# Starting the input projection with two of five token tiles, in a two-layer diffusion step on one core

## The chip, the cores and the metric

The kernel runs on one core of a Trainium2 chip. The metric is the device time of one execution in microseconds (us). The core has five engines that run their own instruction queues in order: TensorE (PE in the rows; PEld is its weight load), VectorE (DVE), ScalarE (ACT), GpSimd (POOL) and SyncE (SP), which issues most of the loads.

## The reference

Two layers work on 128 context tokens and 512 latent tokens of 1024 features. Layer 0 is latent attention, layer 1 a gated MLP. The part that the change touches is the head of layer 0:

```python
def modulation(cond, w_mod, b_mod):
    m = (jax.nn.silu(cond) @ w_mod + b_mod).reshape(-1, 1, 3 * D_MODEL)
    return m[..., :D_MODEL], m[..., D_MODEL:2 * D_MODEL], m[..., 2 * D_MODEL:]
...
        sh_l, sc_l, g_l = modulation(c, w_mod[layer], b_mod[layer])
        hl = rmsnorm(xl, norm_g[layer]) * (1.0 + sc_l) + sh_l
...
def mla_project(h, w_in, q_norm_g, kv_norm_g, w_uq):
    proj = h @ w_in
    c_q = proj[..., :Q_RANK]
    c_kv = proj[..., Q_RANK:Q_RANK + KV_RANK]
```

The input x is normalised per token, scaled and shifted per feature with values that come from the conditioning vector (one set for context, one for latent tokens), and multiplied with w_in. Behind it follow attention, the MLP layer, and a last norm.

## The kernel before

The 640 tokens are five token tiles of 128 (tile 0 is the context), the 1024 features are eight feature tiles. Every matrix product of the projection is made of three float32r products: a matrix is split into a high half (cast on ScalarE) and a low half (the rest, on VectorE) by `split` (L143), and `mm3` (L148) adds high by high, high by low and low by high.

The head works in four kinds of steps.

- The norm of a token tile: squares with their sum on ScalarE (L303), two small steps for the reciprocal root on VectorE and GpSimd (`rstd`, L154), scaling on VectorE (L306).
- Turning: TensorE turns the normalised tile, eight 128x128 blocks per token tile (L316), into `xnT`, where features lie on partitions; ScalarE and VectorE copy it out of PSUM.
- Modulation: the scale and shift of the feature tiles come in six pieces (`PIECES`, L202: four of one feature tile, two of two). `mod_piece` (L213) loads w_mod, 1 MB for one feature tile, and multiplies it with silu(c) (L225); `mod_cols` (L234) copies the resulting rows out of PSUM (L238), turns them with TensorE (L240), reduces them to columns and adds bias and gain (L245, L254, L261). `conditions` (L284) makes silu(c) from rows of all small vectors, which TensorE turns first (L286).
- The projection: `h_piece` (L331) applies scale and shift to the feature tiles of a piece (L337) and splits the result into halves; `load_tok` (L275) loads and splits 832 columns of w_in for one feature tile; `tok_mm` (L353) multiplies one token tile with it, 512 columns (q), and 320 more (kv) for tokens 0 and 1. Five token tiles times eight feature tiles add up in PSUM.

Before the change, the order in the code is: all five x loads among the small rows; the five norms; piece 0 of the modulation and token weights 0; the turning of all five tiles; then for each piece in turn the modulation and h of the *next* piece, ahead of the products of this one:

```python
for q, (k0, nk) in enumerate(PIECES):
    ks = range(k0, k0 + nk)
    if q + 1 < len(PIECES):
        mod_piece(*PIECES[q + 1], True)
        mod_cols(*PIECES[q + 1])
        h_piece(*PIECES[q + 1])
        ...
        for t in range(NT):
            tok_mm(t, ks, 0)
```

The instructions of an engine stand in the order that a scheduling layer makes from this program; each engine works them off in order, waiting where its operands are not there. Loads issued by SP go through eight semaphores in turn: a load waits on SP until the one eight loads earlier has landed, and until the place that it overwrites is free. `raw` and `raw2` are rings of places for loaded weights; `raw2` lies on the places of the x tiles.

Of the kernel before, what the change touches and what calls it, by code (L numbers as in the profile page):

```python
# [9 lines left out]
AF = mybir.ActivationFunctionType  # L10
# [84 lines left out]
def _program(tc, nc, i, o, sb, ps, dr):  # L95
# [22 lines left out]
    def R(a, n):  # L118
        return arR[:, a : a + n]

    def F(a, n):
        return arF[:, a : a + n]
# [11 lines left out]
    def dtile(name):  # L134
        while turn[0] % 4 in held:
            turn[0] += 1
        a = turn[0] % 4 * 1024
        turn[0] += 1
        return arP[:, a : a + 1024]
# [34 lines left out]
    def load_x(t):  # L174
        nc.sync.dma_start(F(F_X + t * D, D), x_src[t])

    def load_rows(name, at, n):
        src = i[name]
        src = (
            src.rearrange("(k p) -> k p", p=P)  # L180
            if len(src.shape) == 1
            else src.rearrange("a (k p) -> (a k) p", p=P)
        )
        nc.sync.dma_start(arF[at : at + n, F_MOD : F_MOD + P], src)

    load_x(0)
    load_rows("c", C_C, 8)
# [1 line left out]
    load_x(1)  # L189
    load_rows("b_mod", C_BMOD, 48)  # L190
    load_rows("norm_g", C_NG, 16)
    load_x(2)
    load_rows("mlp_v_norm_g", C_VG, 16)
    load_rows("mlp_v_norm_b", C_VB, 16)
    load_rows("attn_q_norm_g", C_QG, 4)
    load_x(3)
    load_x(4)
    make_identity(nc, ident)
    V.memset(nhalf, -0.5)

# [12 lines left out]
    def mod_piece(k0, nk, second):  # L213


        n = 2 * nk * P
        for kk in range(2):
            a = (raw2 if second and kk else raw).take(4 * n)
            for part in range(2):
                nc.sync.dma_start(  # L220
                    F3(a, 4 * n, a=4)[:, :, part * nk * P : (part + 1) * nk * P],
                    wmod(0, part * D + k0 * P, nk * P, 4 * kk, 4),
                )
            for j in range(4):
                T.matmul(  # L225
                    arP[32 * j : 32 * j + 32, 3584 : 3584 + n],
                    s32[:, 4 * kk + j, :],
                    F(a + j * n, n),
                    start=kk == 0,
                    stop=kk == 1,  # L230
                    tile_position=(0, 32 * j),
                )
# [40 lines left out]
    wtok = []  # L273

    def load_tok(k):  # L275
        a = (raw2 if k else raw).take(TCOLS)
        nc.sync.dma_start(F(a, TCOLS), i["attn_w_in"][0, k * P : (k + 1) * P, :TCOLS])
        w = ring.take(2 * TCOLS)
        wtok.append((R(w, TCOLS), R(w + TCOLS, TCOLS)))
        if k:  # L280
            split(*wtok[k], F(a, TCOLS))
        return F(a, TCOLS)

    def conditions():  # L284
        pc = dtile("pc")
        T.transpose(pc[:, :C_N], cr[:C_N], ident[:C_N, :C_N])  # L286
        V.tensor_copy(cst, pc[:, :C_N])

        cc = cst[:, C_C : C_C + 16]
        th = col(16)  # L290
        S.activation(th, cc, AF.Tanh, scale=0.5)
        V.scalar_tensor_tensor(silc, th, 1.0, cc, ALU.add, ALU.mult)
        V.tensor_scalar(silc, silc, 0.5, None, ALU.mult)

        V.memset(s32, 0.0)
        V.tensor_copy(s32[:, :, 0:2], silc.rearrange("p (c k) -> p k c", c=2))


    xnT = F3(F_Y, 5120, a=KD)
    for t in range(NT):  # L300
        x = F(F_X + t * D, D)
        ss = col()
        mark = S.activation(F(F_Y + t * D, D), x, AF.Square, accum_out=ss)  # L303
        r = col()
        rstd(r, ss, D)
        V.tensor_scalar(x, x, r, None, ALU.mult)  # L306
        if t == 3:
            with tc.issue_after(mark.ins):
                conditions()
    mod_piece(*PIECES[0], False)  # L310
    first = load_tok(0)
    for t in range(NT):
        x = F(F_X + t * D, D)
        pt = arP[:, t % 3 * 1024 : t % 3 * 1024 + 1024]
        for k in range(KD):
            T.transpose(pt[:, k * P : (k + 1) * P], x[:, k * P : (k + 1) * P], ident)  # L316
        dst = xnT[:, :, t * P : (t + 1) * P]
        pt = pt.rearrange("p (k n) -> p k n", n=P)
        if t == 1:
            V.tensor_copy(dst, pt)  # L320
        elif t > 2:
            S.copy(dst[:, :4], pt[:, :4])
            V.tensor_copy(dst[:, 4:], pt[:, 4:])
        else:
            S.copy(dst, pt)

    def hT(k):
        a = R_HT + k * 1280
# [211 lines left out]
        nc.sync.dma_start(d_gate[layer].rearrange("c k p -> (c k) p"), gro)  # L540


    mod_cols(*PIECES[0])
    h_piece(0, 1, 0, 2)
    split(*wtok[0], first)
    h_piece(0, 1, 2, NT)
    for q, (k0, nk) in enumerate(PIECES):
        ks = range(k0, k0 + nk)
        if q + 1 < len(PIECES):
            mod_piece(*PIECES[q + 1], True)  # L550
            mod_cols(*PIECES[q + 1])
            h_piece(*PIECES[q + 1])
            for k in range(PIECES[q + 1][0], sum(PIECES[q + 1])):
                load_tok(k)
            for t in range(NT):
                tok_mm(t, ks, 0)
                if t < 2:
                    tok_mm(t, ks, 1)
    nc.sync.dma_start(kvg, i["attn_kv_norm_g"].partition_broadcast(P)[:, 0, :])
    for t in range(NT):  # L560
        tok_mm(t, ks, 0)
# [947 lines left out]
```

## Time and profile before

| | |
|---|---|
| runs | 825.76, 826.68, 829.06 us; median 826.68 |
| the profiled execution | 829.0 us; its span from first to last instruction 827.2 us |
| TensorE busy over the span | 801.7 us (97%) |
| VectorE, ScalarE, GpSimd busy | 650.9, 405.5, 44.2 us |
| TensorE's granted clock, mean | 0.995 of full speed |
| loads and stores | 131.13 MB |

The profile is that of one execution. A start in its rows is counted from the start of the span, and a row of a timeline names engine, line, operation and what ended the idle time ahead of it. Pipelined matmuls overlap, so their durations add up to more than the time from one start to the next.

### The profile page before, as it was taken

The numbers are of one execution on the slowest core, as the hardware profiler recorded it, in microseconds if no ns is written. First come the engines' busy times: TensorE is split into PE (matmuls) and PEld (weight loads), VectorE is DVE, ScalarE is ACT, GpSimd is POOL, SyncE is SP. The second block draws the span as 40 slices with busy tenths as digits, with TensorE's granted clock in tenths as the row PEclk, the third lists the DMA queues.
The fourth block names the chain that finished last, engine by engine and source line by source line (L and its number), as shares of the span: only waits on it lengthen the run. The fifth ranks groups of instructions, "written<-read, shape, count | busy, mean of one in ns | idle before, by whom it ended". The sixth has DMA issues, their size and how long they took to land.

```text
span 827.2 us, 12759 instructions
## 1 busy us (share of the span) xinstructions
PE 801.7 (97%) x4874; PEld 732.2 (89%) x4874; DVE 650.9 (79%) x1145; ACT 405.5 (49%) x718; POOL 44.2 (5%) x68
## 2 busy tenths in 40 slices
PE   4999999999999999999999999999999999999996
PEld 3679999999999998887888889899999999888886
DVE  4664998899999798468978759899999997885332
ACT  5334334677666685245322358346564546533111
POOL 1001000000000000001000011100001011200010
PEclk9999999999999999999999999999999999999998
DMA  9981557022115046538869646643444657754111
GB/s 275 333 264 32 179 140 229 2 74 88 57 52 153 3 137 201 193 104 280 257 188 272 192 166 217 199 148 112 128 150 116 188 177 246 251 191 140 64 70 70
DMA packets 105301, 131.13 MB, mean 159 GB/s; under 512 B 5564, under 2 KB 69592, under 8 KB 104984
## 3 DMA queue, kind: packets, MB, share of 16 engines
q1 hardware_dynamic: 102152, 119.77, 46.3%
q0 software_dynamic: 3088, 10.55, 4.0%
q8 instruction: 38, 0.62, 0.3%
q14 instruction: 23, 0.19, 0.1%
HBM read 106.78 MB, written 23.52 MB: 158 GB/s over the span
## 4 chain that ended last, share of the span: by engine, by line
PE 67%; DVE 16%; DMA 9%; issue 5%; ACT 2%; POOL 1%; SPq 0%; POOLq 0%; DVEq 0%; ACTq 0%
PE arP L1218 20%; PE arP L150 13%; PE arP L152 12%; PE arP L151 12%; DVE arR L146 4%; PE arP L756 4%; DVE arF L492 3%; DMA arF<-in_w_mod 3%; DMA arF<-d_h 3%; PE arP L784 1%; PE arP L1275 1%; PE arP L1276 1%; DMA arR<-d_vh 1%; DVE st L768 1%; PE arP L225 1%
## 5 line engine op out<-in xcount | busy, mean ns | idle before, releaser
L150 PE MATMUL arP<-arR 128*128 128x512 f32 (+3 forms) x840 | 298.1, 356 | 1.7 <-DVE arR L146 1.4
L152 PE MATMUL arP<-arR 128*128 128x512 f32 (+3 forms) x840 | 295.8, 353 | 0.0
L151 PE MATMUL arP<-arR 128*128 128x512 f32 (+3 forms) x840 | 295.8, 352 | 0.0
L145 ACT CAST arR<-arF 128x1024 fp32r<-128x1024 f32 (+4 forms) x199 | 164.3, 854 | 160.8 <-PE arP L1218 25.9
L146 DVE TENSOR_TENSOR arR<-arF,arR 128x1024 fp32r<-128x1024 f32 (+4 forms) x199 | 190.4, 974 | 38.0 <-ACT arR L145 33.9
L1218 PE MATMUL arP<-arR 128*128 128x320 f32 x1344 | 202.5, 311 | 0.9 <-DVE arF L1306 0.9
L1218 PEld LDWEIGHTS arP<-arR 128*128 128x128 f32 x1344 | 199.1, 189 | 1.2 <-DVE arF L1306 1.1
L150 PEld LDWEIGHTS arP<-arR 128*128 128x128 f32 x840 | 158.0, 188 | 23.5 <-DVE arR L146 2.6
L152 PEld LDWEIGHTS arP<-arR 128*128 128x128 f32 x840 | 157.9, 188 | 18.4
L151 PEld LDWEIGHTS arP<-arR 128*128 128x128 f32 x840 | 158.0, 188 | 18.1 <-issue 0.8
L492 DVE SCALAR_TENSOR_TENSOR arF<-arF,silc 128x512 f32<-128x512 f32 x112 | 78.4, 743 | 0.8 <-DMA arF<-in_w_mod 0.6
L146 DVE TENSOR_TENSOR arR<-arP,arR 128x512 fp32r<-128x512 f32 (+4 forms) x86 | 54.9, 684 | 9.1 <-ACT arR L145 8.8
L756 PE MATMUL arP<-arR 128*128 128x320 f32 (+1 forms) x360 | 54.9, 309 | 0.2 <-DVE arR L719 0.2
L145 ACT CAST arR<-arP 128x512 fp32r<-128x512 f32 (+4 forms) x86 | 46.0, 605 | 17.4 <-PE arP L152 13.4
L756 PEld LDWEIGHTS arP<-arR 128*128 128x128 f32 x360 | 51.9, 188 | 0.8 <-DVE arR L719 0.4
L772 ACT ACTIVATE arF<-arP,st 128x640 f32<-128x640 f32 (+1 forms) x40 | 28.0, 702 | 14.3 <-DVE st L771 13.9
L1420 DVE TENSOR_TENSOR arF<-arP,arF 128x512 f32<-128x512 f32 (+1 forms) x11 | 6.8, 637 | 33.2 <-PE arP L152 33.2
L157 POOL TENSOR_TENSOR st<-st,nhalf 128x1 f32<-128x1 f32 x15 | 11.0, 734 | 407.6 <-DVE st L156 333.6
L776 ACT ACTIVATE arF<-arF,st 128x640 f32<-128x640 f32 (+1 forms) x40 | 28.9, 742 | 5.2 <-DVE st L775 4.1
L768 DVE TENSOR_REDUCE st<-arP 128x1 f32<-128x640 f32 (+1 forms) x40 | 28.0, 709 | 2.5 <-PE arP L756 2.3
L1422 ACT ACTIVATE arF<-arF 128x512 f32<-128x512 f32 (+1 forms) x11 | 6.5, 589 | 45.4 <-DVE arF L1421 45.4
L1047 ACT ACTIVATE arF<-arP 128x512 f32<-128x512 f32 x20 | 11.7, 592 | 26.4 <-PE arP L152 22.4
(160 smaller groups left out, 698.1 us busy)
## 6 DMA issues: line engine op xcount, KB each, us to landing
arF<-in_mlp_w_in SPq DMA_DIRECT2D x48, 512.0 KB, 4.5
arF<-in_w_mod SPq DMA_DIRECT2D x40, 512.0 KB, 4.8
arF<-in_mlp_w_o SPq DMA_DIRECT2D x32, 256.0 KB, 4.4
d_t<-arF SPq DMA_DIRECT2D x16, 320.0 KB, 3.4
arR<-d_vh POOLq DMA_DIRECT2D x8, 640.0 KB, 6.4
arF<-in_x_sample SPq DMA_DIRECT2D x8, 512.0 KB, 5.2
arF<-in_w_mod SPq DMA_DIRECT2D x16, 256.0 KB, 6.1
arF<-in_attn_w_in SPq DMA_DIRECT2D x8, 512.0 KB, 4.3
```

The costliest lines, as they stand in the source:

```text
L145: S.copy(h, x)
L146: V.tensor_tensor(l, x, h.bitcast(F32), ALU.subtract)
L150: T.matmul(out, a[0], b[0], start=start, stop=False)
L151: T.matmul(out, a[0], b[1], start=False, stop=False)
L152: T.matmul(out, a[1], b[0], start=False, stop=stop)
L492: V.scalar_tensor_tensor(acc[:, c, :], w, sc, acc[:, c, :], ALU.mult, ALU.add)
L756: T.matmul(p[:, n0 : n0 + n], a[:, qs], b[:, c0 : c0 + n], start=s0, stop=s1)
L768: V.tensor_reduce(c[:, 0:1], sc, AX.X if q == 0 else AX.XY, ALU.max)
L772: S.activation(pv, sc, AF.Exp, bias=c[:, 0:1], scale=SCALE, accum_out=c[:, 1:2])
L776: S.activation(pr, pr, AF.Identity, scale=c[:, 2:3])
L1047: S.activation(vt, p, AF.Gelu_apprx_tanh)
L1218: T.matmul(out, x, y, start=first and k + j == 0, stop=k == 3 and j == 2, skip_group_check=True,)
```

## The change

The head is written out in another order, with loads, norms and turning of x spread over it:

- x tiles 2, 3 and 4 are loaded behind w_mod and w_in for feature tile 0 (tile 2) and 1 (tiles 3 and 4).
- Three small row loads go from SP's queue to GpSimd's.
- `mod_piece` becomes a load (`mod_load`) and products (`mod_mm`), so that pieces 1 and 2 can be loaded ahead.
- `x_tile` holds norm and turning of one token tile. Its squares go to a scratch place of `arR`. Every tile is copied out of PSUM in halves by both engines.
- Token tiles 0 and 1 are turned first; feature tile 0 is then multiplied with token tiles 0 to 2, feature tile 1 with token tiles 0 to 2, and both with tiles 3 and 4 at the end. From piece 2 on the loop is the old one.

```diff
     load_rows("b_mod", C_BMOD, 48)
     load_rows("norm_g", C_NG, 16)
-    load_x(2)
-    load_rows("mlp_v_norm_g", C_VG, 16)
-    load_rows("mlp_v_norm_b", C_VB, 16)
-    load_rows("attn_q_norm_g", C_QG, 4)
-    load_x(3)
-    load_x(4)
+    load_rows("mlp_v_norm_g", C_VG, 16, nc.gpsimd)
+    load_rows("mlp_v_norm_b", C_VB, 16, nc.gpsimd)
+    load_rows("attn_q_norm_g", C_QG, 4, nc.gpsimd)
...
     def load_tok(k):
-        a = (raw2 if k else raw).take(TCOLS)
+        a = (raw if k in (0, 2) else raw2).take(TCOLS)
...
-        if k:
+        if k > 2:
             split(*wtok[k], F(a, TCOLS))
...
-    for t in range(NT):
+    scaled = []
+
+    def x_tile(t):
+
         x = F(F_X + t * D, D)
         ss = col()
-        mark = S.activation(F(F_Y + t * D, D), x, AF.Square, accum_out=ss)
+        S.activation(R(R_G + t % 2 * D, D), x, AF.Square, accum_out=ss)
         r = col()
-        rstd(r, ss, D)
-        V.tensor_scalar(x, x, r, None, ALU.mult)
...
+        if t:
+            with tc.issue_after(scaled[-1].ins):
+                rstd(r, ss, D)
+        else:
+            rstd(r, ss, D)
+        scaled.append(V.tensor_scalar(x, x, r, None, ALU.mult))
...
+    at = [mod_load(*PIECES[0], False)]
+    wf = [load_tok(0)]
+    load_x(2)
+    x_tile(0)
+    conditions()
+    x_tile(1)
+    at.append(mod_load(*PIECES[1], True))
+    wf.append(load_tok(1))
+    load_x(3)
+    load_x(4)
+    mod_mm(1, at[0])
     mod_cols(*PIECES[0])
     h_piece(0, 1, 0, 2)
-    split(*wtok[0], first)
-    h_piece(0, 1, 2, NT)
+    split(*wtok[0], wf[0])
+    for t in range(2):
+        tok_mm(t, [0], 0)
+        tok_mm(t, [0], 1)
+    x_tile(2)
+    h_piece(0, 1, 2, 3)
+    tok_mm(2, [0], 0)
+    at.append(mod_load(*PIECES[2], True))
+    wf.append(load_tok(2))
+    mod_mm(1, at[1])
+    mod_cols(*PIECES[1])
+    h_piece(1, 1, 0, 3)
+    split(*wtok[1], wf[1])
+    for t in range(3):
+        tok_mm(t, [1], 0)
+        if t < 2:
+            tok_mm(t, [1], 1)
+    x_tile(3)
+    x_tile(4)
+    h_piece(0, 2, 3, NT)
+    for t in (3, 4):
+        tok_mm(t, [0, 1], 0)
     for q, (k0, nk) in enumerate(PIECES):
+        if q == 0:
+            continue
...
-            mod_piece(*PIECES[q + 1], True)
+            if q == 1:
+                mod_mm(1, at[2])
+                split(*wtok[2], wf[2])
+            else:
+                mod_piece(*PIECES[q + 1], True)
```

How the engines' queues stand after it, at three places. The first is VectorE's queue where the modulation of feature tile 0 becomes columns. First before (L306 scales the last x tile; L320 and L323 copy turned x tiles; L238 copies the rows of modulation piece 0, L245 reduces them; L146 with 128x832 is the low half of token weights 0):

```order
L320 COPY arF<-arP 128x8x128
L306 TENSOR_SCALAR arF<-arF,st 128x1024
L323 COPY arF<-arP 128x4x128
L238 COPY arF<-arP 128x256
L323 COPY arF<-arP 128x4x128
L245 TENSOR_REDUCE modc<-arP 128x2 x2
L254 TENSOR_TENSOR modc<-modc,cst 128x2
L146 TENSOR_TENSOR arR<-arF,arR 128x832
L254 TENSOR_TENSOR modc<-modc,cst 128x2
L261 SCALAR_TENSOR_TENSOR acol<-modc,cst 128x2
```

And of the change, from the low half of token weights 0 to that of h of feature tile 0 for token tiles 0 and 1 (L146 with 128x256; L328 copies a turned x tile, L245 now copies the rows of piece 0 and L252 reduces them, L156 and L320 are the norm's small step and the scaling, here of x tile 2):

```order
L146 TENSOR_TENSOR arR<-arF,arR 128x832
L328 COPY arF<-arP 128x4x128
L245 COPY arF<-arP 128x256
L156 TENSOR_SCALAR st<-st 128x1
L320 TENSOR_SCALAR arF<-arF,st 128x1024
L252 TENSOR_REDUCE modc<-arP 128x2 x2
L261 TENSOR_TENSOR modc<-modc,cst 128x2 x2
L268 SCALAR_TENSOR_TENSOR acol<-modc,cst 128x2
L340 TENSOR_SCALAR arF<-arF,acol,modc 128x128 x2
L328 COPY arF<-arP 128x4x128
L146 TENSOR_TENSOR arR<-arF,arR 128x256
```

The low half of token weights 0 stood behind the reduction of piece 0 and now stands ahead of the copy of its rows; the scaling of x tile 2 now stands between that copy and the reduction.

The second place is TensorE's queue from the last products of feature tiles 0 and 1 to the first of feature tile 2. First before (L225 are the products of modulation piece 3, L240 its turning; the rows ahead of L225 are the products of token tiles 3 and 4 with feature tile 1):

```order
L150 MATMUL arP<-arR 128x512
L151 MATMUL arP<-arR 128x512
L152 MATMUL arP<-arR 128x512
L225 MATMUL arP<-arF 32x256 x8
L150 MATMUL arP<-arR 128x512
L151 MATMUL arP<-arR 128x512
L152 MATMUL arP<-arR 128x512
L150 MATMUL arP<-arR 128x320
L151 MATMUL arP<-arR 128x320
L152 MATMUL arP<-arR 128x320
L240 MATMUL arP<-ident,arF 128x128 x2
```

And of the change (L247 is the turning, of piece 2 the first time and of piece 3 the second; L232 are the products of piece 3):

```order
L150 MATMUL arP<-arR 128x512
L151 MATMUL arP<-arR 128x512
L152 MATMUL arP<-arR 128x512
L247 MATMUL arP<-ident,arF 128x128 x2
L232 MATMUL arP<-arF 32x256 x8
L247 MATMUL arP<-ident,arF 128x128 x2
L150 MATMUL arP<-arR 128x512
L151 MATMUL arP<-arR 128x512
L150 MATMUL arP<-arR 128x320
```

The turning of piece 2 used to stand among the products of feature tile 1, and that of piece 3 among those of feature tile 2; now both stand between the last products of feature tile 1 and the first of feature tile 2.

The third place is the head of SP's queue, as a piece of the difference:

```order
 L184 DMA arF<-in_norm_g 16x128
+L221 DMA arF<-in_w_mod 128x4x128 x4
+L284 DMA arF<-in_attn_w_in 128x832
 L175 DMA arF<-in_x_sample 128x1024
-L184 DMA arF<-in_mlp_v_norm_g 16x128
-L184 DMA arF<-in_mlp_v_norm_b 16x128
-L184 DMA arF<-in_attn_q_norm_g 4x128
+L221 DMA arF<-in_w_mod 128x4x128 x4
+L284 DMA arF<-in_attn_w_in 128x832
 L175 DMA arF<-in_x_sample 128x1024 x2
```

Modulation piece 0 and token weights 0 now go ahead of x tile 2, piece 1 and weights 1 ahead of tiles 3 and 4.

## Rows read from the trace of the kernel before

**Rows 1.** Busy time by stretch: each engine's us (instructions), clock, DMA share, GB/s.

```profile
0.00:9.27 9.27, 0.00 (x0) 0.00 (x0) 1.33 (x5) 4.35 (x6) 1.91 (x8) 1.00 0.78 239
9.27:22.04 12.77, 9.74 (x75) 6.68 (x75) 9.69 (x26) 7.29 (x14) 2.01 (x4) 1.00 1.04 304
22.04:33.56 11.52, 11.52 (x83) 8.42 (x79) 8.62 (x23) 4.41 (x6) 0.00 (x0) 1.00 1.13 329
33.56:60.00 26.44, 26.44 (x148) 19.49 (x145) 16.69 (x42) 9.18 (x14) 0.21 (x1) 1.00 0.90 292
60.00:827.20 767.20, 754.01 (x4579) 697.60 (x4577) 614.60 (x1051) 380.31 (x680) 40.02 (x57) 0.99 0.47 148
```

**Rows 2.** TensorE's timeline, 0 to 34 us: start, duration, line, operation, [idle before, releaser].

```profile
9.27 2.31 PE L316 MATMUL arP<-ident,arF 128*128 128x128 f32 x8 [9.27 <-DVE arF L306]
...
15.71 1.22 PE L316 MATMUL arP<-ident,arF 128*128 128x128 f32 x9
...
22.04 0.50 PE L150 MATMUL arP<-arR 128*128 128x512 f32 x1
22.38 0.39 PE L151 MATMUL arP<-arR 128*128 128x512 f32 x1
22.61 0.40 PE L152 MATMUL arP<-arR 128*128 128x512 f32 x1
...
32.56 1.07 PE L225 MATMUL arP<-arF 128*32 128x256 f32 x16
33.56 0.50 PE L150 MATMUL arP<-arR 128*128 128x512 f32 x1
```

**Rows 3.** The chain that ended last, 0 to 24 us: start, us, what.

```profile
15.23 6.11 DMA arF<-in_w_mod
```

**Rows 4.** The timeline of the other engines, 0 to 24 us.

```profile
2.80 0.42 SPq L184 DMA_DIRECT2D arF<-in_norm_g  x1
...
4.41 1.06 ACT L303 ACTIVATE arF<-arF 128x1024 f32<-128x1024 f32 x1 [2.39 <-DMA arF<-in_x_prompt]
...
5.83 0.55 POOL L157 TENSOR_TENSOR st<-st,nhalf 128x1 f32<-128x1 f32 x1 [4.51 <-DVE st L156]
...
8.47 0.75 DVE L306 TENSOR_SCALAR arF<-arF,st 128x1024 f32<-128x1024 f32 x1
```

**Rows 5.** Instructions by line and form, 0 to 60 us: busy us, mean ns.

```profile
L146 DVE TENSOR_TENSOR arR<-arF,arR 128x832 fp32r<-128x832 f32 x8 | 8.2, 1021 | 0.3 <-ACT arR L145 0.2
...
L145 ACT CAST arR<-arF 128x832 fp32r<-128x832 f32 x8 | 7.1, 887 | 4.6 <-DMA arF<-in_attn_w_in 4.3 <-DMA arF<-in_w_mod 0.2
...
L238 DVE COPY arF<-arP 128x256 f32<-128x256 f32 x4 | 1.7, 422 | 0.9 <-PE arP L225 0.8
...
L323 DVE COPY arF<-arP 128x512 f32<-128x512 f32 x2 | 1.4, 692 | 0.8 <-PE arP L316 0.8
...
L322 ACT COPY arF<-arP 128x512 f32<-128x512 f32 x2 | 1.2, 594 | 1.0 <-PE arP L316 1.0
```

**Rows 6.** Timeline of VectorE and ScalarE, 27 to 33 us, h of feature tile 2.

```profile
29.23 0.23 DVE L245 TENSOR_REDUCE modc<-arP 128x2 f32<-128x8 f32 x2
...
29.89 0.80 DVE L337 TENSOR_SCALAR arF<-arF,acol,modc 128x128 f32<-128x128 f32 x2
...
30.73 0.73 ACT L145 CAST arR<-arF 128x640 fp32r<-128x640 f32 x1 [2.68 <-DVE arF L337]
```

**Rows 7.** DMA issues by line: operation, count, KB each, us to landing.

```profile
arF<-in_norm_g SPq DMA_DIRECT2D x1, 8.0 KB, 4.8
```

**Rows 8.** Loads of d_e from GpSimd's queue: issue ns min/median/max, and landing.

```profile
L1235 POOL DMA_DIRECT2D arF<-d_e x16: 535/552/710, 440.9 to 725.3; - x16
...
DMA to landing us min/median/max: 2.0/4.3/8.1
```

**Rows 9.** Busy time by stretch near the end, columns as in rows 1.

```profile
820.00:822.00 2.00, 0.00 (x0) 0.00 (x0) 1.15 (x4) 0.51 (x2) 0.13 (x1) 1.00 0.00 0
822.00:824.00 2.00, 0.00 (x0) 0.00 (x0) 0.75 (x1) 0.72 (x1) 0.42 (x1) 0.53 0.00 0
```

More of the change, by code (lines that the diff above doesn't have):

```diff
@@ L175, in load_x, with load_rows @@
         nc.sync.dma_start(F(F_X + t * D, D), x_src[t])
-    def load_rows(name, at, n):
+    def load_rows(name, at, n, eng=nc.sync):
         src = i[name]
@@ L183, in load_rows @@
         )
-        nc.sync.dma_start(arF[at : at + n, F_MOD : F_MOD + P], src)
+        eng.dma_start(arF[at : at + n, F_MOD : F_MOD + P], src)
     load_x(0)
@@ L213, in mod_piece, with mod_load @@
     def mod_piece(k0, nk, second):
+        return mod_mm(nk, mod_load(k0, nk, second))
+    def mod_load(k0, nk, second):
         n = 2 * nk * P
+        at = []
         for kk in range(2):
@@ L223, in mod_piece, with mod_mm @@
                 )
+            at.append(a)
+        return at
+    def mod_mm(nk, at):
+        n = 2 * nk * P
+        for kk in range(2):
             for j in range(4):
@@ L227, in mod_piece @@
                     s32[:, 4 * kk + j, :],
-                    F(a + j * n, n),
+                    F(at[kk] + j * n, n),
                     start=kk == 0,
@@ L284, in conditions @@
     def conditions():
-        pc = dtile("pc")
+        pc = arP[:, 3584:4096]
         T.transpose(pc[:, :C_N], cr[:C_N], ident[:C_N, :C_N])
@@ L299, in _program @@
     xnT = F3(F_Y, 5120, a=KD)
-    for t in range(NT):
+    scaled = []
+    def x_tile(t):
         x = F(F_X + t * D, D)
         ss = col()
-        mark = S.activation(F(F_Y + t * D, D), x, AF.Square, accum_out=ss)
+        S.activation(R(R_G + t % 2 * D, D), x, AF.Square, accum_out=ss)
         r = col()
-        rstd(r, ss, D)
-        V.tensor_scalar(x, x, r, None, ALU.mult)
[L307 to L314, printed above, removed]
+        if t:
[4 more added lines that the diff above has]
+        scaled.append(V.tensor_scalar(x, x, r, None, ALU.mult))
+        a = (0, 1024, 1024, 1536, 1536)[t]
+        pt = arP[:, a : a + 1024]
         for k in range(KD):
@@ L318, in _program @@
         pt = pt.rearrange("p (k n) -> p k n", n=P)
[L319 to L325, printed above, removed]
+        S.copy(dst[:, :4], pt[:, :4])
+        V.tensor_copy(dst[:, 4:], pt[:, 4:])
     def hT(k):
@@ L553, in _program @@
             for k in range(PIECES[q + 1][0], sum(PIECES[q + 1])):
[L554 to L558, printed above, removed]
+                if k > 2:
+                    load_tok(k)
+            if q > 1:
+                for t in range(NT):
+                    tok_mm(t, ks, 0)
+                    if t < 2:
+                        tok_mm(t, ks, 1)
     nc.sync.dma_start(kvg, i["attn_kv_norm_g"].partition_broadcast(P)[:, 0, :])
```

## The prediction, made before the change was run

> **What bounds the kernel now.** I read the sum over the span first, then the table by stretch, then TensorE's timeline of the first 40 us, and at last the rows of the other engines that TensorE waits for there. The table by stretch covers the whole span of 827.2 us and shows where time can be won or lost [rows 1]. The execution itself took 829.0 us, so 1.8 us lie around the span; it stands 2.3 us above the median of the runs, 826.68. TensorE does nothing until 9.27. From there to 22.04 it is busy for 9.74 of 12.77 us, from 22.04 to 33.56 for 11.52 of 11.52, to 60 for 26.44 of 26.44, and afterwards for 754 of 767. So the kernel is bound by TensorE, and behind 22.04 nothing takes up a delay: an early or late TensorE moves the end by as much. Only the first 22 us hold a reserve of 12.3 us (9.27 and 3.03), which is what the change could win from.
>
> Two places on TensorE's timeline are my landmarks [rows 2]. The first product of feature tile 0 starts at 22.04, the first of feature tile 2 at 33.56. Between them are all five token tiles of features 0 and 1 and the modulation products of two pieces, with no gap. Up to 33.56 before and up to the same product after, TensorE has done nearly the same work: 40 turnings of x, four modulation pieces, and the products of features 0 and 1. So the change's price is the time at which feature 2 starts.
>
> **The loads.** Up to 9.27 the DMAs moved 239 GB/s, up to 22.04 304 GB/s, behind it 329 [rows 1]. That is 2.22 MB at 9.27 and then 0.30 MB per us. The second half of w_mod's piece 1 is the last of 5.2 MB in the old queue. By this rate its bytes have passed at 9.27 + 2.98 / 0.304 = 19.1; the chain has it landing at 15.23 + 6.11 = 21.34 [rows 3]. So a load lands some two us behind its bytes. In the new order x tile 2 stands behind w_mod piece 0 (1.05 MB) and token weights 0 (0.43 MB), and x 3 and 4 behind piece 1 and weights 1. With x tiles of 0.52 MB, weights 0 end at 2.57 MB, x 2 at 3.1, piece 1 at 4.14, x 3 at 5.1. I take them to land at 12.2, 13.8, 17.4 and 20.5 (estimates, half a us early or late each).
> The queue behind them is safe. Piece 1's second half is loaded over x 0, weights 1 over x 1, piece 2's second half over x 2, piece 3's over x 3, weights 3 over x 4; each waits on SP for the turning of that tile, with all later loads behind it. The worst is weights 3 (x 4's turning, about 30), and piece 4's second part, which waits for the products of piece 3 (about 36). At the 6.1 us of that load [rows 3] it is there by 43, when feature 2's products end. This costs nothing; it would with 2 us less.
>
> **The new order, step by step.** Durations are from [rows 2, 4, 5, 6].
> (a) The turning of the conditions now heads TensorE's queue, and x 0 and x 1 stand behind it. It wants norm_g, issued on SP at 2.80 and 4.8 us under way [rows 4, 7]: 7.6. x 0 is scaled by then: 5.83 + 0.55 for the power, 0.75 for the scaling, 7.2, where before it ran at 8.47, behind x 1's first step. Eight turnings took 2.31 at the start, 0.14 each later (nine in 1.22); two tiles end at 11.8 or so, piece 0's products (1.07) at 12.9. This gains 1.4 us at the front and bounds nothing.
> (b) VectorE meets the wait. Its queue has the low half of weights 0 ahead of x 1's copy and of the copy of piece 0's rows: 12.2, ScalarE's cast 0.89, the low half 1.02, then a half-tile copy and the 256-wide copy, 0.69 and 0.42, less a tenth or so for overlap at their ends: 15.15.
> (c) Next in VectorE's queue is x 2, ahead of piece 0's reduction. x 2 lands at 13.8; from the start of the squares to the power took 1.42 (4.41 to 5.83), 15.2 here and 15.4 because VectorE's step between them waits for (b); the power 0.55, the scaling 0.75: 16.75. Then reduction, sums and gain, 0.66 (29.23 to 29.89), and two modulations, 0.6 (0.80 for five tiles): 18.0. TensorE turns x 2 meanwhile; ScalarE copies half of it (0.59) and casts h (0.4, where five tiles take 0.73): 18.6. The first product starts at 18.6, **3.4 us earlier** than before.
> (d) Tiles 0 to 2 of feature 0: nine wide products at 0.23 (22.38 to 22.61) and six narrow at 0.15 (320 of 512 columns) make 2.97, and 0.4 for the low half of h. With the rest of piece 1, 22.4.
> (e) VectorE copies the rows (0.4 behind 0.25 of drain) and scales x 3 (0.75): 23.7. Turning it 1.1, half of piece 2 0.55, h of feature 1 0.3: 25.65. Three tiles of feature 1, 2.97: 28.6.
> (f) Turning x 4 and the rest of piece 2: 30.3. Now TensorE has only tiles 3 and 4 of features 0 and 1, whose h needs x 4 copied (0.69), modulated (0.3) and cast (0.4): 31.4. Twelve products at 0.23: 34.2.
> (g) Feature 2 needs h for all tiles, and its modulation is turned only now, behind those twelve: 0.55 with the drain. In VectorE's queue follow reduction and a sum (0.45), the low half of weights 3 (1.0), sums and gain (0.3), the copy of piece 3's rows (0.4), h (0.80), and on ScalarE the cast (0.73): 34.75 + 3.7 = **38.5**. Before, the same chain ran under 21 products of the feature ahead. TensorE has only piece 3 (1.07) to fill it.
> Against 33.56 that is 4.9 us late. Two turnings of piece 3, 0.3, are then already done: **4.6 us slower**.
> So TensorE's start moves from 9.27 to 7.6 and the first product by 3.4 us, but the work that used to hide each next h is used up. The waits come back: 1.6 in (e), 1.1 in (f), 2.6 in (g), beside 3.7 between 12.9 and 18.6.
> The rest is priced at nothing: the squares' new scratch place and the fixed PSUM place of the conditions have the same size; x's copies in halves (0.59 and 0.69 side by side) are in (c), (e) and (f). Behind feature 3 all engines have the old order, but for one small load on SP.
>
> **Two costs in doubt.** The three row loads moved to GpSimd stand ahead of the identity in its queue. The only loads of before from there that are near in size took 0.55 us to issue and 4.3 to land, the slowest 8.1 [rows 8]. Three issues from 0.74 end at 2.4, so the rows are there at 6.7, ahead of norm_g, or at 10.5.
> TensorE's granted clock is 1.00, its 2.4 GHz level, in every stretch before 60 [rows 1]. It falls to 0.53 on average in 822 to 824, going to its 1.2 GHz level after two us in which the engine had nothing to do [rows 9]. The new order has TensorE nearly idle from 12.9 to 16.7 (only two turnings). If the clock falls there, the work up to about 20 (x 2's turning, piece 1, the first products) may take twice its time, as the first eight turnings did against the later ones (0.29 and 0.14 each [rows 2]): 1.6 us more. The Trainium skill's "TensorE: Matmul & The Clock Gate" (Part 1: The HAM clock gate) says that an idle array goes to half rate and that activity brings it back; by that rule the sum would be 6.2. Against it stands 9.27: after nine idle us the row says 1.00 [rows 1].
>
> **Rivals.**
> - *The waits are covered* (not slower; 0.20). If h is ready whenever TensorE asks, its own work from 18.6 on counts: 2.97, 0.4, 0.4, 1.1, 0.55, 2.97, 1.1, 0.55, 2.8, 0.3, 1.07, together 14.2, so feature 2 at 32.8. That is 0.8 early, 1.1 with the two turnings: 826.7 - 1.1 = 825.6. It decides where (g) shrinks from 3.7 to under 1. For it: VectorE is busy for 8.62 of 11.52 us [rows 1]. Against it: the chain in (g) is one of dependences, row by row, and not of load.
> - *Loads early and waits covered* (0.05). With weights 0 and x 2 landing ahead of 10, (b) and (c) start at the end of x 1's scaling, 10, instead of 12.2 and 13.8, and the first product some 2.5 us sooner still: 823, barely within the bound; only more would be over it. The rates [rows 1] speak against it.
> - *The clock falls* (0.15): 4.6 + 1.6, 832.9.
> - *The rows come late* (0.10): if they land at 10.5 instead of before 7.6, piece 0's products end at 15.8 instead of 12.9 and (b) at 16.1; 1.0 more, 832.3.
>
> **The numbers.** The forecast has the remaining 0.50: 829.0 + 4.6 = 833.6 for an execution like the profiled one, and 826.7 + 4.6 = **831.3** against the median. Its own range, with loads half a us either way and VectorE's chains up to a us shorter, is 829.7 to 832.7. The whole range reaches from the covered waits, less what the runs differ by, to the clock with late rows: 825.0 to 835.0. A measurement tells 0.5%, 4.1 us, from no change. The forecast's own range straddles this: 0.36 of its 0.50 lie beyond. With the clock (0.15) and most of the late rows (0.07), slower has 0.58, the same 0.37, faster 0.05.
>
> **What would show it.** On TensorE's timeline: the conditions' turning near 7.6, the first wide product near 18.6, the first of feature 1 near 25.7, a gap of about 1 near 30.3 released by ScalarE's cast, and one or two together 2 to 3 us long ahead of feature 2 near 38.5, released by VectorE and ScalarE. The table by stretch from 60 on should have the same sums as before. I am wrong if feature 2 starts before 35, or if a late feature 2 does not move the end.

## The result, and the profile after

The changed kernel takes 832.0 us (median of five runs, 830.6 to 832.95) against 826.63 for the kernel before in the same session: ratio 1.0068, 95% interval 1.0050 to 1.0087. It is slower by 5.6 us, and the lower end of the interval is just at the 0.5% that the prediction took as its bound. The point forecast was 831.3. The profiled execution took 832.88 us, its span 831.1.

The table by stretch, cut at the same times as [rows 1]: each engine's us (instructions), clock, DMA share, GB/s.

```profile
0.00:9.27 9.27, 0.82 (x4) 0.85 (x5) 1.59 (x7) 3.62 (x6) 2.98 (x10) 1.00 0.84 242
9.27:22.04 12.77, 10.42 (x58) 6.30 (x57) 8.48 (x24) 7.13 (x13) 1.65 (x3) 0.87 1.06 338
22.04:33.56 11.52, 9.66 (x67) 6.62 (x66) 6.93 (x19) 3.47 (x8) 0.55 (x1) 1.00 0.73 214
33.56:60.00 26.44, 24.49 (x145) 16.87 (x144) 17.37 (x48) 8.60 (x11) 0.00 (x0) 1.00 0.87 281
60.00:831.10 771.10, 758.70 (x4608) 701.27 (x4606) 616.84 (x1056) 382.25 (x686) 39.89 (x57) 1.00 0.47 149
```

TensorE was busy without a gap from 22.04 to 60 before [rows 1]; now it is idle for 1.86 us up to 33.56 and for 1.95 behind it. In 9.27 to 22.04 it is busy for 0.7 longer than before, but at a mean clock of 0.87 instead of 1.00.

TensorE's timeline up to feature 2, to be laid beside [rows 2] (start, duration, line, operation, count, [idle before, what ended it]). L293 turns the conditions, L324 an x tile, L232 is a modulation product, L247 turns modulation rows.

```profile
8.45 0.43 PE L293 MATMUL arP<-ident,arF 116*128 116x116 f32 x1 [8.45 <-DMA arF<-in_norm_g]
8.67 4.03 PE L324 MATMUL arP<-ident,arF 128*128 128x128 f32 x16
12.63 1.94 PE L232 MATMUL arP<-arF 128*32 128x256 f32 x16
15.64 0.44 PE L247 MATMUL arP<-ident,arF 128*128 128x128 f32 x2 [1.08 <-DVE st L156]
17.21 1.23 PE L324 MATMUL arP<-ident,arF 128*128 128x128 f32 x8 [1.13 <-DVE modc L252]
18.36 1.92 PE L232 MATMUL arP<-arF 128*32 128x256 f32 x10
20.21 0.80 PE L150 MATMUL arP<-arR 128*128 128x512 f32 x1
...
25.06 0.44 PE L247 MATMUL arP<-ident,arF 128*128 128x128 f32 x2 [0.54 <-DVE arF L245]
...
27.50 0.50 PE L150 MATMUL arP<-arR 128*128 128x512 f32 x1
...
33.16 0.50 PE L150 MATMUL arP<-arR 128*128 128x512 f32 x1 [0.97 <-ACT arR L145]
...
36.02 0.38 PE L247 MATMUL arP<-ident,arF 128*128 128x128 f32 x2
36.73 1.07 PE L232 MATMUL arP<-arF 128*32 128x256 f32 x16 [0.33 <-DVE modc L252]
38.39 0.44 PE L247 MATMUL arP<-ident,arF 128*128 128x128 f32 x2 [0.59 <-DVE arF L245]
39.86 0.50 PE L150 MATMUL arP<-arR 128*128 128x512 f32 x1 [1.03 <-ACT arR L145]
```

The first product starts at 20.21 instead of 22.04, feature 2 at 39.86 instead of 33.56: 1.8 us ahead has become 6.3 behind. The waits that the prediction named are there, released by VectorE and ScalarE, and each group is shorter than forecast: 0.76 us ahead of feature 1 (forecast 1.6; a wait of 0.22 at 25.72 is left out above), 0.97 ahead of tiles 3 and 4 (1.1), and 1.95 in three pieces ahead of feature 2 (2.6).

The clock, in the table by stretch at one us each:

```profile
17.00:18.00 1.00, 0.79 (x7) 0.82 (x8) 0.93 (x8) 0.13 (x1) 0.00 (x0) 0.99 1.02 408
18.00:19.00 1.00, 1.00 (x11) 0.42 (x10) 0.77 (x2) 1.00 (x3) 0.00 (x0) 0.50 0.96 380
...
21.00:22.00 1.00, 1.00 (x7) 0.86 (x6) 0.15 (x1) 0.97 (x3) 0.54 (x1) 0.80 1.19 308
22.00:23.00 1.00, 1.00 (x7) 0.87 (x7) 0.00 (x0) 0.37 (x2) 0.00 (x1) 1.00 1.09 267
```

From 18.0 to about 21.4 the granted clock is 0.50, the 1.2 GHz level. Ahead of that TensorE had done two turnings between 14.57 and 17.21. The work up to 21.4 is five products of piece 1, which take 1.85 to the next instruction, and the first wide products, of which the first lasts 0.80 (0.50 in [rows 2]).

Behind the head the delay is passed on. The prediction expected the sums from 60 on to stay; counted from 60 they can't, because work that stood ahead of 60 now falls behind it. The first turning of the projected rows, which follows the last product of the projection, starts at 72.00; before, it started at 65.95:

```profile
72.00 0.38 PE L405 MATMUL arP<-ident,arF 128*128 128x128 f32 x2
```

This start, 6.05 late, is the landmark for all runs below. Behind it the sums are the same, as the prediction said: 4543 matmuls on TensorE in both, busy for 748.06 us before and 746.70 now, VectorE for 612.77 and 612.47. The spans of the two profiled executions differ by less, 3.9 us; that of before was the longest of its runs (829.0 against a median of 826.7). Compare the landmark with the ratio times 826.7: for ten of the eleven kernels they agree within 1.1 us.

```
kernel                     landmark, us late   (ratio - 1) x 826.7
changed kernel                  6.05                 5.6
e1_clock_kept                   5.72                 5.6
e2_ahead                        4.42                 2.6
e3_clock_and_ahead              1.67                 1.7
e4_products_first               4.38                 4.1
e5_low_half_later               4.23                 4.1
e6_clock_and_low_half           3.32                 3.8
e7_rewritten_order              6.50                 5.5
e8_rewritten_and_clock          7.09                 8.1
e9_norms_behind                 3.89                 3.6
e10_norms_and_clock             4.24                 4.6
```

### The profile page after: what moved, and what is told of

Its sections match the earlier page's. It is cut to its first block, busy times and chain, and to the rows that moved or that the text cites. A ratio compares the mean times of both kernels' runs of the same rounds, so it can differ in the third digit from the quotient of the medians.

```text
span 831.1 us, 12770 instructions
## 1 busy us (share of the span) xinstructions
PE 804.1 (97%) x4874; PEld 731.9 (88%) x4874; DVE 651.2 (78%) x1151; ACT 405.1 (49%) x721; POOL 45.1 (5%) x71
## 5 line engine op out<-in xcount | busy, mean ns | idle before, releaser
L145 ACT CAST arR<-arF 128x1024 fp32r<-128x1024 f32 (+6 forms) x201 | 164.3, 848 | 155.9 <-PE arP L152 25.0
L146 DVE TENSOR_TENSOR arR<-arF,arR 128x1024 fp32r<-128x1024 f32 (+6 forms) x201 | 190.0, 965 | 38.8 <-ACT arR L145 35.3
L146 DVE TENSOR_TENSOR arR<-arP,arR 128x512 fp32r<-128x512 f32 (+4 forms) x86 | 54.9, 683 | 8.3 <-ACT arR L145 8.1
L1090 ACT ACTIVATE arF<-arP 128x512 f32<-128x512 f32 x20 | 11.7, 591 | 26.4 <-PE arP L152 17.6
```

Source lines behind the costliest of these rows:

```text
L145: S.copy(h, x)
L146: V.tensor_tensor(l, x, h.bitcast(F32), ALU.subtract)
L1090: S.activation(vt, p, AF.Gelu_apprx_tanh)
```

## The experiments

All are edits of the changed kernel, timed against the kernel before in the same session; so ratios are compared, not times. Beside its edit each keeps the order of the head, unless it is said.

**The clock kept.** Idle turnings of the identity fill TensorE's thin stretch.

```diff
+    def fill(ins, n):
+        with tc.issue_after(ins.ins):
+            for _ in range(n):
+                T.transpose(arP[:, 3072:3200], ident, ident)
...
-    mod_mm(1, at[0])
+    fill(mod_mm(1, at[0]), 7)
```

(and 4 more behind the turning of piece 0's rows.)

> The changed kernel with 11 idle turnings of the identity on TensorE, 7 behind modulation piece 0's products and 4 behind the turning of its rows; all other work keeps its order on every engine. Theory (waits and a lost clock): the granted clock stays at 1.00 from 17 to 22, piece 1's first products take 0.13 each instead of 0.27, the first product starts near 19.0 instead of 20.2, feature 2 near 38.3 instead of 39.9, and the time is 1.5 us below the changed kernel, 830.5, ratio to before 1.0048. Rival (the clock costs nothing, since h of tiles 0 and 1 is cast only at 18.8 and the scaling of x 3 waits for ScalarE): the clock may read 1.00, but feature 2 stays at 39.9 within 0.4 and the time at 832. If the clock still falls, the run says nothing about its price.

Measured: ratio 1.0068 (1.0049 to 1.0087), no change against the changed kernel. Yet in the front the mechanism worked. The clock reads 1.00 in every stretch from 14 to 26, and from the turning of piece 0's rows to feature 1 it now takes 10.25 us (14.50 to 24.75) instead of 11.86 (15.64 to 27.50); the five products of piece 1 take 0.98 of it. That is 1.6 less, the price that the prediction gave the clock. In the profiled execution it was lost again behind the twelve products. TensorE's timeline:

```profile
24.75 0.50 PE L150 MATMUL arP<-arR 128*128 128x512 f32 x1
...
33.27 0.38 PE L248 MATMUL arP<-ident,arF 128*128 128x128 f32 x2
33.98 1.07 PE L232 MATMUL arP<-arF 128*32 128x256 f32 x16 [0.33 <-DVE modc L255]
36.68 0.44 PE L248 MATMUL arP<-ident,arF 128*128 128x128 f32 x2 [1.63 <-DVE arF L246]
38.15 0.79 PE L150 MATMUL arP<-arR 128*128 128x512 f32 x1 [1.03 <-ACT arR L145]
```

From the end of the twelve products to feature 2 it takes 4.88 us, 1.04 more than in the changed kernel (36.02 to 39.86). SP's queue, ScalarE and VectorE show why, one row of each:

```profile
28.57 0.34 SPq L292 DMA_DIRECT2D arF<-in_attn_w_in  x1
34.09 0.89 ACT L145 CAST arR<-arF 128x832 fp32r<-128x832 f32 x1 [3.41 <-DMA arF<-in_attn_w_in]
35.00 1.02 DVE L146 TENSOR_TENSOR arR<-arF,arR 128x832 fp32r<-128x832 f32 x1 [0.95 <-ACT arR L145]
```

The same load and cast in the changed kernel:

```profile
31.32 0.34 SPq L284 DMA_DIRECT2D arF<-in_attn_w_in  x1
34.64 0.89 ACT L145 CAST arR<-arF 128x832 fp32r<-128x832 f32 x1 [1.21 <-DMA arF<-in_attn_w_in]
```

Weights 3 overwrite x 4, so their load leaves only when x 4 is turned. The low half of weights 3 stands in VectorE's queue between the two sums of feature 2's columns. The columns come 2.75 earlier than in the changed kernel (33.27 against 36.02), and the load leaves 2.75 earlier too (28.57 against 31.32). But it takes 5.5 us until the cast here and 3.3 there, so VectorE waits 0.95 with the rest of the columns behind it. x 4's turning is therefore not what made it late. The trace records the landing of a load in sixteen parts: fifteen of this one had landed by 31.87, the last at 34.06; in the changed kernel the last two landed at 34.42 and 34.62. Why one part was late no run shows. Then the clock fell at the second place:

```profile
36.00:38.00 2.00, 0.44 (x2) 0.20 (x2) 1.89 (x12) 0.63 (x1) 0.00 (x0) 0.95 1.02 349
38.00:40.00 2.00, 1.85 (x5) 1.66 (x6) 2.00 (x4) 1.40 (x3) 0.00 (x0) 0.50 0.95 328
```

The products of feature 2 start at 0.50, and from their first to the products of piece 4 it takes 5.92 us instead of 4.54. In sum: 1.6 won, 1.0 and 1.4 given back; this execution's loads were also 1.1 earlier (14.50 against 15.64), and its landmark is 0.33 earlier. The rival was right on the time, but not on feature 2, which came 1.7 earlier and not within 0.4. The six executions lie at 830.7 to 831.4 (three) and 833.4 to 834.4 (three), and the profiled one, 833.45, is of the longer ones. Whether the shorter ones lost the gain in the same way is not shown.

**The lookahead given back.** Piece 2 and h of feature 2 stand ahead of the twelve products again.

```diff
     x_tile(4)
+    mod_mm(1, at[2])
+    mod_cols(*PIECES[2])
     h_piece(0, 2, 3, NT)
+    split(*wtok[2], wf[2])
+    h_piece(*PIECES[2])
     for t in (3, 4):
         tok_mm(t, [0, 1], 0)
```

> The changed kernel with the lookahead given back at the last place only: modulation piece 2's products, turning, columns and h of feature 2 stand ahead of the twelve products of token tiles 3 and 4. Theory (the cover is used up): the first of the twelve products starts some 0.4 later, as VectorE copies piece 2's rows ahead of h of tiles 3 and 4 (33.6 instead of 33.2), the chain to h of feature 2 then runs under them, only piece 3's products (1.07) stand between them and feature 2, and feature 2 starts near 37.5 instead of 39.9; the time is 2.3 us below the changed kernel, 829.7. Rival (loads: weights of feature 2 landed only at 34.6 and piece 3 of w_mod later still, so the loads set feature 2's start): feature 2 at 39 or later, the time within 0.8 us of 832.

Measured: ratio 1.0032 (1.0018 to 1.0047), 3.0 us below the changed kernel, and clear of its interval. TensorE's timeline:

```profile
33.68 0.50 PE L150 MATMUL arP<-arR 128*128 128x512 f32 x1 [0.32 <-ACT arR L145]
...
36.63 1.07 PE L232 MATMUL arP<-arF 128*32 128x256 f32 x16
37.63 0.50 PE L150 MATMUL arP<-arR 128*128 128x512 f32 x1
```

Behind the twelve products only piece 3's own 1.0 us is left, instead of 3.84; from feature 1 to the twelve it takes 0.34 more. That is the theory: from feature 1 to feature 2 it takes 9.95 us instead of 12.36, 2.4 less, as forecast. That feature 2 also starts within 0.15 of the forecast 37.5 is in part luck. In this execution the clock fell earlier (0.69 in 15 to 16, then 0.50 to 22), which cost 1.3 more than in the changed kernel, and the loads came 1.1 earlier. The first of these hides part of the gain in its landmark.

**Both.** The last two edits together.

> Both edits together, the idle turnings and the lookahead for piece 2. Theory: two separate costs, which add up: feature 2 near 36.0, 3.8 us below the changed kernel, 828.2, still 1.5 above before. Rival (one common bound, the loads or VectorE): no more than the better of the two alone.

Measured: ratio 1.0020 (1.0004 to 1.0037), the best of all variants, and still above 1. TensorE's first wide product, the first of feature 2, and the landmark:

```profile
18.25 0.50 PE L150 MATMUL arP<-arR 128*128 128x512 f32 x1
...
35.00 0.50 PE L150 MATMUL arP<-arR 128*128 128x512 f32 x1
...
67.62 0.38 PE L413 MATMUL arP<-ident,arF 128*128 128x128 f32 x2
```

The two costs are separate and add up. Feature 2 is 4.9 earlier than in the changed kernel: 1.1 from loads that came earlier in this execution, 1.4 up to feature 1 (10.49 from the turning of piece 0's rows instead of 11.86), and 2.4 from there on (9.97 instead of 12.36). It is still 1.4 later than before. What is left are waits of 0.54, 0.22, 0.57 and 0.32 us ahead of feature 1 and of the twelve products, 1.65 in all; the landmark is 1.67 late. The first product comes 3.8 earlier than before, but from it to feature 2 TensorE has 15.1 us of work beside the waits, where before it had 11.5, because turning and modulation that stood ahead of the first product now stand behind it. So with every wait covered this order would start feature 2 at 33.35, only 0.2 ahead of before.

**Products first.** The steps of x 2 are held back, so that the products of tiles 0 and 1 come first, as written in the code.

```diff
+    hb = h_piece(0, 1, 0, 2)
...
-    x_tile(2)
+    x_tile(2, hb, pb)
...
+    with tc.issue_after(pb.ins):
+        mod_mm(1, at[1])
```

(`x_tile` puts its small step behind `hb` on VectorE and its turning behind `pb`, the last product of tile 1, on TensorE. The scheduling layer then also turns x 4 ahead of feature 1's products.)

> The changed kernel with the written order kept at feature 0: x 2's small step and scaling behind h of tiles 0 and 1 on VectorE, x 2's turning and modulation piece 1's products behind the twelve products of tiles 0 and 1 on TensorE. Theory: piece 0's reduction starts right behind its turning, 16.1, instead of 17.0; h of tiles 0 and 1 is cast at 17.7 and the first product starts there instead of at 20.2; TensorE is idle from 16.1 to 17.7 and may lose its clock as before, so some 1.0 to 1.5 of these 2.5 us go into half-rate products. x 2 comes later by what TensorE does first, and the chains in front of features 1 and 2 stay: feature 2 0.8 to 1.5 earlier, 38.4 to 39.1, the time 831. Rival (only the front's order was wrong): feature 2 at 37.3 or earlier, 2.5 us below the changed kernel.

Measured: 830.91 us, ratio 1.0049 (1.0033 to 1.0064), 1.6 below the changed kernel, with intervals that overlap. The first product comes at 17.02, 3.2 earlier than in the changed kernel, at a clock of 0.50 until 20.5. Feature 2 starts at 37.63, which is better than the theory's 38.4 and near the rival's 37.3. The reason is not the front alone: x 4 is turned early, so the twelve products follow without a wait, and weights 3's low half no longer stands among the sums, so that from the end of the twelve to feature 2 it takes 2.69 instead of 3.84. The time is near the theory's.

**The low half moved away.** One instruction on VectorE.

```diff
+        if k == 3:
+            S.copy(wtok[k][0], F(a, TCOLS))
+            with tc.issue_after(h2.ins):
+                V.tensor_tensor(wtok[k][1], F(a, TCOLS), wtok[k][0].bitcast(F32), ALU.subtract)
```

(`h2` is the last modulation of feature 2's h.)

> The changed kernel with one instruction moved on VectorE: the low half of weights 3 (1.02), which stands between the two sums of piece 2's columns, is issued behind h of feature 2. Theory: it lies in the chain ahead of feature 2, so feature 2 starts 1.0 earlier, near 38.9, and the time is 1.0 below the changed kernel, 831, ratio to before 1.0056. Rival (the chain's length is set by piece 3's rows and the casts, not by VectorE's queue): feature 2 stays at 39.9.

Measured: ratio 1.0050 (1.0035 to 1.0065), 1.5 below the changed kernel, with intervals that overlap; the trace is the clearer of the two. TensorE's timeline:

```profile
35.36 0.38 PE L247 MATMUL arP<-ident,arF 128*128 128x128 f32 x2
...
38.06 0.50 PE L150 MATMUL arP<-arR 128*128 128x512 f32 x1
```

From the end of the twelve products to feature 2 it takes 2.70, so 1.14 less; expected was 1.0.

**The clock kept and the low half moved away.**

> The kernel with the idle turnings, which kept its clock and had feature 1 2.75 early but feature 2 only 1.7, and lost the rest at 1.2 GHz behind it, with the same low half of weights 3 moved behind h of feature 2. Theory (the gain was given back at the load of weights 3, which waits for x 4's turning and has no cover left): without the half in the way, which started 0.95 late and took 1.02, feature 2 starts near 36.2 instead of 38.15, the wait is short enough for the clock to stay at 1.00 (1.4 more), and the time is 3.3 below that kernel, 829, ratio 1.003. Rival (the front's gain never reaches the end, whatever stands at feature 2): the time stays at 832.

Measured: ratio 1.0046 (1.0025 to 1.0067). TensorE's timeline:

```profile
33.94 0.38 PE L248 MATMUL arP<-ident,arF 128*128 128x128 f32 x2
...
36.27 0.44 PE L248 MATMUL arP<-ident,arF 128*128 128x128 f32 x2 [0.55 <-DVE arF L246]
36.64 0.50 PE L150 MATMUL arP<-arR 128*128 128x512 f32 x1
```

From the end of the twelve products to feature 2 it takes 2.70 instead of 4.88, and feature 2 runs at 1.00 (4.54 to piece 4, as in the changed kernel). The landmark is 2.4 earlier than with the idle turnings alone, although this execution's front was 0.7 later. But two things differ between these two executions. Here the load of weights 3 landed whole, 3.4 us after it left:

```profile
29.24 0.34 SPq L292 DMA_DIRECT2D arF<-in_attn_w_in  x1
32.65 0.89 ACT L296 CAST arR<-arF 128x832 fp32r<-128x832 f32 x1 [1.30 <-DMA arF<-in_attn_w_in]
```

So in this execution the half would not have waited for it even at its old place, and the move would be worth what it is without the idle turnings, 1.14. The times, 828.5 to 838.0, are 1.8 below those with the idle turnings alone and 0.3 below those with the half moved alone; neither is clear of the intervals. That the clock's gain reaches the end once the half is out of the way is seen in this landmark, 0.9 earlier than with the half moved alone, and not shown by the times.

**A new order.** Four kernels, all with the new loads, try to cover every wait: products of tiles 0 and 1 first, tile 2 of feature 0 behind piece 1's products, x 3 and x 4 turned between the token tiles of feature 1, piece 2 ahead of the twelve products. In the second pair the norms of x 3 and x 4 are held behind h of feature 1; the second of each pair has 15 idle turnings.

```diff
+    pb, sq = x_tile(2, hb, pb)
+    with tc.issue_after(pb.ins):
+        pb = mod_mm(1, at[1])
+    with tc.issue_after(pb.ins):
+        pb = tok_mm(2, [0], 0)
...
+    h1 = h_piece(1, 1, 0, 3)
+    tok_mm(0, [1], 0)
+    pb = tok_mm(0, [1], 1)
-    pb, _ = x_tile(3, None, pb, sq)
+    pb, _ = x_tile(3, h1, pb, sq)
```

(the last two lines are the step from the first pair to the second.)

> The new loads with another order of work, in which each wait is covered: the rows of piece 0 are copied ahead of the low half of weights 0; the products of tiles 0 and 1 run before x 2's turning and piece 1's products; tile 2 of feature 0 behind piece 1's products, so that it covers its columns; x 3 and x 4 turned between the token tiles of feature 1; piece 2's products, columns and h of feature 2 ahead of the twelve products of tiles 3 and 4. No idle turnings. Theory: first product near 16, with the clock probably at 1.2 GHz from there to 20 or so, since TensorE is idle from 13 to 16 but for two turnings; one wait of about 1 ahead of feature 1; feature 2 near 33 to 34, and the time within 1 of before, 826 to 828. Rival (loads set the pace: x 3 lands at 20.5, piece 2's second half 6 behind x 2's turning): waits of several us on loads between features 0 and 2, feature 2 at 35 or later, 828.5 or more.

> The same order with 15 idle turnings ahead of the first product (5 behind piece 0's products, 10 behind the turning of its rows). Theory: the clock stays at 1.00, feature 2 1 to 1.7 earlier than without them, 32 to 33 against 33.56 before, and the time 0.5 to 1.5 below before, ratio 0.998 to 0.9995. Rival (loads): no earlier than without them.

Measured: ratios 1.0067 (1.0048 to 1.0086) and 1.0098 (1.0074 to 1.0122). Both theories failed; the first rival's figures (feature 2 at 35 or later, 828.5 or more) came true, but not by loads. TensorE and VectorE of the first:

```profile
26.14 0.80 PE L150 MATMUL arP<-arR 128*128 128x512 f32 x1 [3.49 <-ACT arR L145]
...
24.21 0.75 DVE L340 TENSOR_SCALAR arF<-arF,st 128x1024 f32<-128x1024 f32 x1 [0.38 <-POOL st L157]
24.88 0.66 DVE L364 TENSOR_SCALAR arF<-arF,acol,modc 128x128 f32<-128x128 f32 x2
```

Feature 1 waits 3.49. On VectorE the scaling of x 3 stands ahead of the columns of piece 1 and that of x 4 between these columns and h (L364), and each waits for GpSimd; behind it the clock falls to 0.50 until about 32. And x 4, turned at 32.1, lets the loads behind it go later. With the idle turnings feature 1 waits as long (3.50); feature 2 starts 0.6 earlier (38.37 against 38.94), but the products of piece 4 start at 44.71, 0.6 later, behind a wait of 1.51.

> The rewritten order with the norms of x 3 and x 4 moved behind h of feature 1 on VectorE; there they had stood between the reduction of piece 1 and h of feature 1, waiting for GpSimd, and feature 1 came 3.5 late and the clock fell behind it. Theory: feature 1 starts near 24 instead of 26.1, the clock stays at 1.00 there, x 4 is turned by 28 instead of 33 and the load of weights 3 leaves 4 earlier; feature 2 near 34 instead of 38.9, and the time about 4.5 below that kernel, 828, within 1 of before. Rival (the new loads hold it back in any order): a wait of 2 or more for x 3, x 4 or piece 2's second half, feature 2 at 36 or later, 830 or more.

> The same with the 15 idle turnings ahead of the first product. Theory: first product 0.7 earlier and no half-rate products, if there were any; feature 2 near 33.2, the time 827, level with before. Rival: what is won ahead of feature 1 is waited for there, no change against the kernel without the idle turnings.

Measured: ratios 1.0044 (1.0027 to 1.0062) and 1.0056 (1.0041 to 1.0071). Feature 1 starts at 24.06, as forecast, but waits 1.97 for h, and the clock still falls behind it. x 4 is turned at 29.12 and not by 28. SP's queue, ScalarE and TensorE of the first:

```profile
29.86 0.34 SPq L293 DMA_DIRECT2D arF<-in_attn_w_in  x1
...
35.17 1.51 ACT L145 CAST arR<-arF 128x832 fp32r<-128x832 f32 x2 [3.21 <-DMA arF<-in_attn_w_in]
...
36.74 0.50 PE L150 MATMUL arP<-arR 128*128 128x512 f32 x1 [0.72 <-ACT arR L145]
```

The load of weights 3 leaves behind x 4's turning and lands 5.3 later, again with one late part (fifteen of sixteen by 33.43, the last at 35.15); its cast stands on ScalarE ahead of that of h of feature 2, and feature 2 starts at 36.74, behind a wait of 0.72. The rival's figures came true, but its cause only with this 0.72. In the kernel with idle turnings the load landed 3.3 after it left, and feature 2 starts at 36.90 without a wait. Up to there its trace shows the waits of 1.02, 0.47 and 1.97 up to feature 1, one of 0.38 behind its first products, and the clock at 0.50 from about 26 to 29. The idle turnings change nothing for the better: in the kernel without them the clock was 1.00 from 14 to 24 anyway.

## Why the prediction was right, and where its sizes were off

The mechanism was right. The start was won, and then the h of later features became waits, since the work that had hidden them was used up. The run with the lookahead given back shows it at the costliest place: the same chain, put under the twelve products, no longer costs anything but piece 3's 1.0. Step by step:

- **(a)** Forecast 7.6, measured 8.45, released by norm_g as said. That it bounds nothing holds: the first step of VectorE's chain is the cast of weights 0, released by its load at 12.71 (forecast 12.2). From that cast to the turning of piece 0's rows it takes 2.93 here, and 2.93 and 2.93 in two runs whose conditions were turned at 7.39 and 7.28 (11.63 to 14.56, 11.26 to 14.19). The late rows on GpSimd did not come about: they landed in 3.8 to 4.7 us.
- **(b), (c)** The turning of piece 0's rows starts at 15.64 (forecast 15.15), the scaling of x 2 ends at 17.06 (16.75). The cast of h starts at 18.36, but the first product at 20.21 and not 18.6. The step that failed is the one to "18.6": x 2's turning and five products of piece 1 stand ahead of it on TensorE, and these products ran at 0.50. In the three runs with idle turnings in this order it takes 3.47 to 3.71 from the turning of the rows to the first product, 4.57 in the changed kernel, 3.45 in the forecast; so the clock is nearly the whole difference. That the forecast's 3.45 fits is in part luck: it ends with the cast of h, which with the clock kept is done at about 17.6, while the first product then waits in TensorE's queue behind piece 1 until 17.98.
- **(d), (e), (f)** From the first product to the end of tiles 0 to 2: 4.31 (forecast 3.8, and 3.79 with the clock kept). From there to feature 1: 2.98 (3.25). The three tiles 3.08 (2.95). From their end to the twelve products 2.58 (2.8), with the wait of 0.97 on ScalarE's cast (forecast 1.1).
- **(g)** 3.84 (forecast 4.3). The low half of weights 3, counted in it with 1.0, is worth 1.14 by the run that moves it.
- **The sum.** Feature 2 was forecast 4.9 late and came 6.3 late: 0.5 from the loads, 1.6 from the clock, less 0.8 in (e) to (g). Of the 0.3 that the prediction takes off behind it, the landmark shows 0.25. So the point forecast, 831.3, lies nearer to the measured 832.0 than its terms do; errors of both signs cancelled. The interval of the time, 4.1 to 7.2 us slower, holds the forecast with the clock and without it, and only the trace tells them apart.

So the likeliest case was forecast without the clock, and the rival "the clock falls" came true with it. Its price, 1.6, is that of this execution; two others paid 2.4 and 2.9 (last section). Its chance, 0.15, was too low: in all three traces of this order without idle turnings the clock fell ahead of the first product. The argument against it, that the row says 1.00 after nine idle us, does not hold for this place: the clock fell at 18.0 with TensorE at work again since 17.2. The Trainium skill's "TensorE: Matmul & The Clock Gate" (Part 1: The HAM clock gate), by which the sum would be 6.2, is borne out in kind: the granted clock fell behind the thin stretch and was back at 1.00 from 22. Its 6.2 stands beside 5.6 in the time and 6.05 at the landmark.

The load of weights 3, which the prediction priced at nothing, costs nothing in the changed kernel: it is cast at 34.64, and its low half has its turn only at 36.71. In two of the other traces it cost something: 0.95 on VectorE with the idle turnings and 0.72 on TensorE in the new order with the norms held back, both times with one part of the load landing about 2 us behind the rest. The prediction's other rival, the covered waits, took 14.2 us of work from the first product to feature 2; the run with both edits had 15.1.

Open is what would make this start pay. In the order of the run with both edits there is little left to win: 0.2 us at feature 2 with every wait covered. The new orders bring the first product to 15.4 to 16.2 and lost this lead to VectorE's queue and to the clock, and in one trace 0.72 to the load of weights 3. An order with other places for weights 3 was not tried.

## What to carry to other kernels

Where an engine is busy without a gap behind a certain point, an earlier start is worth nothing by itself: ask for each later chain what work hid it, and whether that work is still there when the chain runs. Ask also whether the work that stood ahead of the early start has only moved behind it. A cure at the first wait can show as no change in the time; look at a landmark behind each step before calling it free. One trace is one execution: what took the gain there may be missing in the next one. A half or a cast that nobody needs yet, placed inside a chain of an engine's queue, passes the lateness of its load on to the chain (0.95 us of wait and 1.02 of work with the idle turnings).

## What the runs showed of the hardware

- The clock's fall differs between executions of the same order. In the changed kernel it reads 0.99 in 17 to 18 and 0.50 from 18; in the kernel with the low half moved, whose order up to there is the same, 0.54 already in 14 to 15:

```profile
14.00:15.00 1.00, 0.69 (x2) 0.29 (x2) 0.34 (x3) 0.00 (x0) 0.55 (x1) 0.54 1.18 318
```

  From the turning of piece 0's rows to feature 1 this makes 12.7 us there (14.19 to 26.88), 13.1 with the lookahead given back (14.56 to 27.68), 11.9 in the changed kernel, 10.25 with the clock kept. So the price of a fall was between 1.6 and 2.9 us at the same place.
- No single idle time of TensorE ahead of the fall at 18.0 was longer than 1.13 us; it was two idle times, 1.08 and 1.13, with two turnings between them. In the new order with the norms held back, and without idle turnings, there is one of 2.18 ahead of 15.4, and the clock stayed at 1.00 until 24.
- The row of the granted clock says 1.00 in 8 to 13, while the sixteen turnings there took 4.03 us, 0.25 each; at 0.50 eight took 1.81 to 1.94 in the runs above, at 1.00 later 1.03. So the first turnings take about as long as at 0.50, and the row does not show it. Why is not shown.
- One of the sixteen parts of a load can land well behind the others. Of the load of weights 3 the last part came 2.19 us behind the fifteenth with the idle turnings and 1.72 in the new order with the norms held back, but 0.19 in the changed kernel and 0.06 with the idle turnings and the low half moved.
